# Attention in a two-layer trunk: seven of the second mixer's eight groups in a hand-written order, each taken in two parts by query tile, with the first output unit's split inside

## The chip, the cores and the metric

The kernel runs on one core of one Trainium2 chip. The metric is the device time of one execution in microseconds, taken as the median of several runs. The core has a matmul engine (PE, whose weight load shows as PEld), a vector engine (DVE), a scalar engine (ACT), GpSimd (POOL) and SyncE (SP, which here only issues DMAs). Each engine works through its own list of instructions in order and waits where an operand or a free buffer is late.

## The reference

A denoising trunk of two layers over 128 context tokens and 256 latent tokens, 1024 wide, all in float32. Each layer is a gated feed-forward half-step, a mixer, and another feed-forward half-step. The mixer of layer 0 is latent attention with 8 heads beside a convolution; that of layer 1, the second mixer, is grouped-query attention with 16 query heads of 64 over 4 key and value heads. Context tokens attend to the context alone; latent tokens attend to a cache of 128 keys and the 256 latent keys, and the kernel computes both at once.

```python
def block_attention(q, k, v, scale):
    ...
    def one(qblk):
        s = jnp.einsum('bqhgd,bshd->bhgqs', qblk, k).astype(jnp.float32) * scale
        p = jax.nn.softmax(s, axis=-1).astype(v.dtype)
        return jnp.einsum('bhgqs,bshd->bqhgd', p, v)
...
def gqa_mixer(h, w_in, g_q, g_k, w_out, ctx):
    B, S, _ = h.shape
    q, k, v = jnp.split(h @ w_in, [MIX_C, MIX_C + GQA_KV_HEADS * GQA_HEAD_DIM], axis=-1)
    q = rms_norm(q.reshape(B, S, GQA_HEADS, GQA_HEAD_DIM), g_q)
    k = rms_norm(k.reshape(B, S, GQA_KV_HEADS, GQA_HEAD_DIM), g_k)
    ...
    o = block_attention(q.reshape(B, S, GQA_KV_HEADS, grp, GQA_HEAD_DIM), keys, vals, GQA_HEAD_DIM ** -0.5)
    return o.reshape(B, S, MIX_C) @ w_out, (k, v)
```

## The kernel before, in words

All 384 tokens are worked on together, with features on the partitions. The stages follow one another: feed-forward, first mixer (`mixer_a`), two feed-forwards, second mixer (`mixer_c`), feed-forward, store.

**Dense products.** A weight matrix comes in units of 128x2048 values by DMA into a ring of three raw tiles. Each unit is split in two halves of 128x1024 into a rounded part (ACT, L162) and a remainder (DVE, L174; some units of `mixer_a` instead take ACT's L171 and a DMA that adds). Activations are split likewise: ACT casts the high part (L631), DVE subtracts it for the low part (L632). One product is then three matmuls (L264 to L266). There are four halves of each kind, so a split waits until the matmuls of an earlier unit are through. `stream` walks a list of such units: it splits up to two units ahead, calls a unit's matmuls, and after the next unit's matmuls were listed its `post`.

**Attention.** `attention` takes the heads two at a time, a group: four groups in `mixer_a`, eight in `mixer_c`. For a group of two heads the steps are:

- *scores* (L665): for each head the three query tiles of 128 rows. Tile 0 and tile 1 are latent rows against 384 keys, tile 2 is the context rows against 128. Tiles 0 and 2 of a head share one PSUM buffer, tile 1 has its own.
- *softmax*: a row maximum for each tile and head on DVE (L680, six), its product with the negated norm (L682, four), the exponentials on ACT, which also give the row sums (L685, six), and one reciprocal of all sums on DVE (L687).
- *pv*: the probabilities are turned on PE, per head four and three transposes (L703, L707) into `ps_tr` and `ps_ax` buffers, copied out by ACT (L705, 128x512) and, in `mixer_c`, by DVE (L709, 128x384); the reciprocals are turned and spread by twelve small matmul passes (L466) and copied out (L713, DVE in `mixer_c`); eight value matmuls (L719) into `ps_ax`, and DVE multiplies them by the reciprocals (L722) into a temporary `t`, which is split into `MXh` (L631) and `MXl` (L632), the input of the output product.

PSUM has four `ps_mm` buffers, two `ps_tr` and two `ps_ax`. The two heads' probabilities lie in `pr` tiles, of which `mixer_c` has four, and their turned form in `pt` tiles, of which it has two.

**Order.** A tile scheduler orders each engine's list, by the order of the program and by what it estimates to be ready; inside a `manual_schedule` block it keeps the order as written. The code before has no such block in attention. In `mixer_c` the product that makes queries, keys and values has six units. Group 0's scores and softmax come inside unit 4 (`first`), its `pv`, with group 1's scores (`ahead`) and softmax, inside unit 5 (`group`); groups 1 to 7 follow through `rest`: the scores of group g+1, then the `pv` of group g, then the softmax of group g+1. After them `out_steps` makes four units of the output product, the first two with the raw tiles loaded and split by the stream as buffers allow. In `mixer_a` all four groups go through `rest`, beside a convolution on DVE (L920) and its layer norm (L1004, L1007, L1010, L1026, L1029), which gives the other half of the input of its output product.

Of the kernel before, what the change touches and what calls it, by code (L numbers as in the profile page):

```python
# [6 lines left out]
F32 = mybir.dt.float32  # L7
# [8 lines left out]
P = 128  # L16
# [5 lines left out]
T = 384  # L22
# [57 lines left out]
class Trunk:  # L80
# [95 lines left out]
    def stream(self, steps):  # L176
        depth = {"raw": NRAW, "rawm": NRAWM}
        rest = {r: deque(s for s in steps if s.ap is not None and s.ring == r) for r in depth}
# [21 lines left out]
        done_split = set()  # L200
# [442 lines left out]
    def attention(self, heads, pairs, pool=None):  # L643

        nc = self.nc
        S = {}
        room = []

# [8 lines left out]
        def scores(hs):  # L657
            for h in hs:
                S[h] = (self.ps_mm(), self.ps_mm())
            for dst, c0, cols, q0 in ((0, 0, slice(0, T), 0), (0, T, slice(T, 512), TL), (1, 0, slice(0, T), P)):  # L660
                for h in hs:
                    qT, kT, rows = heads[h][:3]
                    kw = {"tile_position": (rows.start, 0)} if pairs else {}
                    n = cols.stop - cols.start
                    nc.tensor.matmul(S[h][dst][:, c0:c0 + n], lhsT=qT[rows, q0:q0 + P], rhs=kT[rows, cols],  # L665
                                     start=True, stop=True, **kw)

        Pm, Rm = {}, {}

        def softmax(hs):  # L670

            mx, sm = self.tb("mx", 6, 4), self.tb("sm", 6, 4)
            prs = [scratch(0, h) for h in hs]
            part = lambda h, i: (S[h][0][:, 0:T], S[h][1][:, 0:T], S[h][0][:, T:512])[i]
            off = (0, T, 2 * T, 7 * P)
            for ids in ((0, 2), (1,)):
                for j, (h, pr) in enumerate(zip(hs, prs)):
                    sc, nsc = heads[h][4], heads[h][5]
                    for i in ids:
                        nc.vector.reduce_max(out=mx[:, 2 * i + j:2 * i + j + 1], in_=part(h, i), axis=AX.X)  # L680
                    c, cj = slice(ids[0], 3, 2), slice(2 * ids[0] + j, 6, 4)
                    nc.vector.tensor_tensor(out=mx[:, cj], in0=mx[:, cj], in1=nsc[:, c], op=ALU.mult)  # L682
                    for i in ids:
                        k = slice(2 * i + j, 2 * i + j + 1)
                        nc.scalar.activation(pr[:, off[i]:off[i + 1]], part(h, i), AF.Exp, scale=sc[:, i:i + 1],  # L685
                                             bias=mx[:, k], accum_out=sm[:, k])
            nc.vector.reciprocal(sm, sm)  # L687
            Rm[hs[0]] = sm
            for h, pr in zip(hs, prs):
                S.pop(h)  # L690
                Pm[h] = pr

        def pv(hs, MXh, MXl, ps=None):

            pts = []
            for h in hs:
                pr = Pm.pop(h)
                pt = scratch(1, h).rearrange("p (a b) -> p a b", b=P)
                pts.append(pt)
                ta, tb = (ps or (self.ps_ax if h == hs[1] else self.ps_tr))(), (ps or self.ps_tr)()  # L700
                for kt in range(2):
                    for qb in range(2):
                        nc.tensor.transpose(ta[:, (2 * kt + qb) * P:(2 * kt + qb + 1) * P],  # L703
                                            pr[:, qb * T + kt * P:qb * T + kt * P + P], self.ident)
                nc.scalar.copy(pt[:, 0:4, :], ta.rearrange("p (a b) -> p a b", b=P))  # L705
                for i, o in enumerate((2 * P, T + 2 * P, 2 * T)):
                    nc.tensor.transpose(tb[:, i * P:i * P + P], pr[:, o:o + P], self.ident)  # L707
# [614 lines left out]
```

## Time and profile before

| what | value |
|---|---|
| median of three runs | 1467.29 us (1466.56 to 1467.69) |
| the profiled execution | 1467.06 us |
| its span in the trace | 1465.3 us, so 1.76 us lie around it |
| mean granted PE clock | 0.996 |
| PE busy | 1438.0 us (98%) |
| DVE busy | 1156.5 us (79%) |
| ACT busy | 667.7 us (46%) |
| groups 1 to 7 of the second mixer | about 1090 to 1140 us from the span's start |
| first matmul of the second mixer's output product | 1139.49 us |

A row of the trace's timeline gives the start, the duration, engine, line, operation, output and input, and how often it repeats without a break; behind it, in square brackets, stands how long the engine was idle before it and what ended this. Durations of one engine can overlap a little, since an instruction starts before the one ahead of it has drained; so the distance from one start to the next is what it costs in a row of equal ones. A matmul in float32 shows as two records.

### The profile page before, as it was taken

How to read it: one execution, taken by the hardware profiler on the slowest of the kernel's cores; microseconds unless marked ns; L12 is line 12 of the kernel's file. 1: busy time of each engine (PE TensorE's matmuls, PEld its weight loads, DVE VectorE, ACT ScalarE, POOL GpSimd, SP SyncE). 2: the span in 40 equal slices, each digit the busy share in tenths (PEclk: the TensorE clock that was granted, in tenths of full speed). 3: DMA queues.
4: the chain of work that ended last, by engine and by line, in shares of the span. 5: the costliest groups of instructions: out<-in, count | busy, mean ns of one | idle time of the engine just before them, and what ended most of it. 6: DMA issues, size and time to landing. Idle time of an engine off the chain costs nothing. (4 is left out here: it accounts for less than half of the span.)

```text
span 1465.3 us, 22131 instructions
## 1 busy us (share of the span) xinstructions
PE 1438.0 (98%) x8450; PEld 1397.6 (95%) x8450; DVE 1156.5 (79%) x2411; ACT 667.7 (46%) x1177; POOL 26.1 (2%) x36
## 2 busy tenths in 40 slices
PE   8999999999999999999999999999998999999997
PEld 6999999999889999999999999999976999999997
DVE  5899999959987999999779996445887698555443
ACT  4534333368776434343344333333477443333332
POOL 0000000021100000000000000000000000000000
PEclk9999999999999999999999999999999999999998
DMA  9665657699656566657565662334310263432341
GB/s 384 247 226 208 231 186 256 240 239 216 152 141 229 182 231 221 212 203 244 201 232 206 230 225 97 107 131 163 128 59 30 87 230 144 140 119 90 117 134 48
DMA packets 45066, 262.55 MB, mean 179 GB/s; under 512 B 4992, under 2 KB 6816, under 8 KB 22048
## 3 DMA queue, kind: packets, MB, share of 16 engines
q1 hardware_dynamic: 38592, 245.04, 46.6%
q0 software_dynamic: 4032, 14.16, 5.2%
q10 hardware_dynamic: 2336, 1.94, 0.4%
q8 instruction: 67, 1.10, 0.3%
q14 instruction: 39, 0.32, 0.1%
HBM read 244.98 MB, written 1.98 MB: 169 GB/s over the span
## 5 line engine op out<-in xcount | busy, mean ns | idle before, releaser
L162 ACT CAST whi<-raw 128x1024 fp32r<-128x1024 f32 (+1 forms) x346 | 327.9, 948 | 579.5 <-PE ps_mm L266 507.4
L264 PE MATMUL ps_mm<-Hh,wlo 128*128 128x386 f32 x1568 | 533.7, 340 | 0.8 <-DMA wlo<-raw 0.8
L265 PE MATMUL ps_mm<-Hl,whi 128*128 128x386 f32 x1568 | 530.6, 338 | 0.0
L266 PE MATMUL ps_mm<-Hh,whi 128*128 128x386 f32 x1568 | 529.7, 338 | 0.0
L174 DVE TENSOR_TENSOR wlo<-raw,whi 128x1024 fp32r<-128x1024 f32 (+2 forms) x318 | 346.4, 1089 | 154.5 <-ACT whi L162 152.0
L264 PEld LDWEIGHTS ps_mm<-Hh,wlo 128*128 128x128 f32 x1568 | 295.4, 188 | 3.1 <-PE ps_mm L266 1.1
L265 PEld LDWEIGHTS ps_mm<-Hl,whi 128*128 128x128 f32 x1568 | 295.8, 189 | 0.5
L266 PEld LDWEIGHTS ps_mm<-Hh,whi 128*128 128x128 f32 x1568 | 294.8, 188 | 0.0
L265 PE MATMUL ps_mm<-Gl,whi 128*128 128x384 f32 x704 | 236.7, 336 | 0.0
L264 PE MATMUL ps_mm<-Gh,wlo 128*128 128x384 f32 x704 | 236.7, 336 | 0.0
L266 PE MATMUL ps_mm<-Gh,whi 128*128 128x384 f32 x704 | 236.7, 336 | 0.0
L378 DVE SCALAR_TENSOR_TENSOR junk<-rawm,eb 128x1024 bf16<-128x1024 f32 x128 | 156.2, 1220 | 1.0 <-ACT eb L143 1.0
L378 DVE SCALAR_TENSOR_TENSOR rawm<-rawm,eb 128x1024 f32<-128x1024 f32 x128 | 156.1, 1219 | 0.3
L264 PEld LDWEIGHTS ps_mm<-Gh,wlo 128*128 128x128 f32 x704 | 132.0, 187 | 0.0
L265 PEld LDWEIGHTS ps_mm<-Gl,whi 128*128 128x128 f32 x704 | 132.0, 187 | 0.0
L266 PEld LDWEIGHTS ps_mm<-Gh,whi 128*128 128x128 f32 x704 | 132.0, 187 | 0.0
L631 ACT CAST Gh<-g 128x384 fp32r<-128x384 f32 x88 | 45.1, 512 | 89.2 <-DVE g L547 89.2
L540 ACT ACTIVATE sa<-ta,ba 128x256 f32<-128x256 f32 (+1 forms) x176 | 70.3, 447 | 3.8 <-DVE ta L537 3.7
L920 DVE SCALAR_TENSOR_TENSOR acc<-ub,vec,acc 128x399 f32<-128x399 f32 x120 | 69.8, 628 | 0.3
L547 DVE SCALAR_TENSOR_TENSOR g<-t,bb,sa 128x256 f32<-128x256 f32 (+1 forms) x176 | 65.4, 413 | 0.4 <-ACT sa L540 0.4
L485 DVE SCALAR_TENSOR_TENSOR X<-ps_mm,mod,X 128x256 f32<-128x256 f32 x88 | 32.7, 412 | 39.1 <-PE ps_mm L266 39.1
L632 DVE TENSOR_TENSOR Gl<-g,Gh 128x384 fp32r<-128x384 f32 x88 | 49.0, 557 | 12.3 <-ACT Gh L631 12.2
(276 smaller groups left out, 1285.6 us busy)
## 6 DMA issues: line engine op xcount, KB each, us to landing
raw<-wi SPq DMA_DIRECT2D x85, 1024.0 KB, 4.8
rawm<-wmt SPq DMA_DIRECT2D x64, 1024.0 KB, 4.8
raw<-wo SPq DMA_DIRECT2D x64, 704.0 KB, 4.0
wlo<-raw POOLq DMA_DIRECT2D x24, 512.0 KB, 6.3
raw<-wia SPq DMA_DIRECT2D x7, 1024.0 KB, 7.9
raw<-wic SPq DMA_DIRECT2D x6, 1024.0 KB, 4.8
raw<-wm SPq DMA_DIRECT2D x5, 1024.0 KB, 14.4
raw<-woc SPq DMA_DIRECT2D x4, 1024.0 KB, 4.9
```

Source lines behind the costliest of these rows:

```text
L162: self.nc.scalar.copy(hi, s.raw[:, c0:c1])
L174: self.nc.vector.tensor_tensor(out=lo, in0=raw, in1=hi.bitcast(F32), op=ALU.subtract)
L264: mm(out, lhsT=lo, rhs=rh, start=start, stop=False)
L265: mm(out, lhsT=hi, rhs=rl, start=False, stop=False)
L266: mm(out, lhsT=hi, rhs=rh, start=False, stop=stop)
L378: self.nc.vector.scalar_tensor_tensor(out=junk, in0=raw[:, i], scalar=1.0, in1=self.eb[:, c], op0=ALU.mult, op1=ALU.mult, accum_out=out[:, ...
L485: nc.vector.scalar_tensor_tensor(out=self.X[:, d, s0:s1], in0=ps[:, s0:s1], scalar=gate[:, d, c:c + 1], in1=self.X[:, d, s0:s1], op0=ALU.m ...
L540: nc.scalar.activation(sa[:, s0:s1], ta[:, s0:s1], AF.Silu, bias=ba[:, c:c + 1])
L547: nc.vector.scalar_tensor_tensor(out=g[:, s0:s1], in0=t2[:, s0:s1], scalar=bb[:, c:c + 1], in1=sa[:, s0:s1], op0=ALU.add, op1=ALU.mult)
L631: self.nc.scalar.copy(hi, src)
L632: self.nc.vector.tensor_tensor(out=lo, in0=src, in1=hi.bitcast(F32), op=ALU.subtract)
L920: nc.vector.scalar_tensor_tensor(out=acc[j], in0=src(t), scalar=w(t), in1=acc[j], op0=ALU.mult, op1=ALU.add)
```

## The change

`attention` is rewritten in smaller steps, each by group g and part b. Part 0 holds query tiles 0 and 2, part 1 holds tile 1: `scores(g, b)` (now L675), `maxima(g, b)` (L690, then one product L692 for both heads), `exps(g, b)` (L698), `recip(g)` (L704), `turn(g, b)` (transposes L715, copies L718), `sums(g)` (the turned reciprocals, L467, and their copy L724), `values(g)` (L734, the product L737, the cast L739), and the low part L740 that `values` hands back to be called later. Beside the order:

- part 0 is turned into `ps_tr` for both heads and copied by ACT, part 1 into `ps_ax` and copied, in `mixer_c`, by DVE; the values go to `ps_tr` (group 0 of `mixer_c`: `ps_ax`);
- the copy of the turned reciprocals goes from DVE to ACT in `mixer_c`;
- two products of maxima and norms per group stand where there were four;
- in `mixer_c` groups 1 to 7 run through `laid`, under `manual_schedule`;
- the first raw tile of the output product is loaded ahead of `laid`, and its two halves are split inside: the first at the end of group 6's turn, the second within group 7's; `stream` passes over a unit that has its tile and its halves.

`mixer_a` uses the new steps through `rest`, ordered by the tile scheduler. The lists of the feed-forwards, SP and POOL are the same as before. DVE has 32 instructions fewer, ACT 8 more, PE the same number.

```diff
+        def maxima(g, b):
...
+            for j, h in enumerate(hs):
+                for i in ids[b]:
+                    nc.vector.reduce_max(out=mx[:, i, j:j + 1], in_=part(h, i), axis=AX.X)
+            c = (slice(0, 3, 2), slice(1, 2))[b]
+            nc.vector.tensor_tensor(out=mx[:, c], in0=mx[:, c], in1=heads[hs[0]][5][:, c], op=ALU.mult)
...
+        def turn(g, b, ps=None):
+
+            for j, h in enumerate(groups[g]):
...
+                p = (ps or (self.ps_tr, self.ps_ax)[b])()
+                src = ((0, P, 2 * P, 2 * T), (T, T + P, T + 2 * P))[b]
+                for i, o in enumerate(src):
+                    nc.tensor.transpose(p[:, i * P:i * P + P], Pm[h][:, o:o + P], self.ident)
+                n = len(src)
+                copy = nc.vector.tensor_copy if pool and b else nc.scalar.copy
+                copy(pts[g][j][:, b:7:2, :], p[:, 0:n * P].rearrange("p (a b) -> p a b", b=P))
+
+        def sums(g, ps=None):
+            p = (ps or self.ps_tr)()
+            self.turn_rows(p, Rm.pop(g))
+            R = Rm[g] = self.tb("g")
+            nc.scalar.copy(R, p[:, 0:T])
+
+        def values(g, MXh, MXl, ps=None):
...
+            on = self.tb("t2")
+            nc.vector.tensor_tensor(out=on, in0=o[:, 0:T], in1=Rm.pop(g), op=ALU.mult)
+            i = heads[hs[0]][6]
+            nc.scalar.copy(MXh[:, i, :], on)
+            return lambda: nc.vector.tensor_tensor(out=MXl[:, i, :], in0=on, in1=MXh[:, i, :].bitcast(F32),
+                                                   op=ALU.subtract)
...
+        def laid(g0, MXh, MXl, unit):
+
+            low = lambda: None
+            with self.tc.manual_schedule():
+                for g in range(g0, len(groups)):
+                    more = g + 1 < len(groups)
+                    if more:
+                        scores(g + 1, 0)
+                    turn(g, 0)
+                    if more:
+                        maxima(g + 1, 0)
+                    low()
+                    sums(g)
+                    if more:
+                        exps(g + 1, 0)
+                        scores(g + 1, 1)
+                    turn(g, 1)
+                    if more:
+                        maxima(g + 1, 1)
+                    else:
+                        self.split_half(unit, 1)
+                    low = values(g, MXh, MXl)
+                    if more:
+                        exps(g + 1, 1)
+                        recip(g + 1)
+                    if g + 2 == len(groups):
+                        self.split_half(unit, 0)
+                low()
...
             self.stream(steps)
-            rest(MXh, MXl, 1)
-            self.stream(self.out_steps(a["woc"], MXh, MXl, lambda: self.mods[l, GM], nxt))
+            outs = self.out_steps(a["woc"], MXh, MXl, lambda: self.mods[l, GM], nxt)
+            outs[0].raw = self.rawp.tile([P, UN], F32, tag="raw", name="raw", bufs=NRAW)
+            nc.sync.dma_start(out=outs[0].raw, in_=outs[0].ap)
+            laid(1, MXh, MXl, outs[0])
+            self.stream(outs)
```

The lists of the engines show it at three places. First PE, from the end of one group's values to the end of the next's, in the middle of the second mixer; in each row stand the line, the operation, output and input with buffer numbers, the shape, and how many follow. `cst` is the identity, `pr` the probabilities (or, as a factor of `Vt`, their turned form), `sm` the reciprocals. Before:

```order
L665 MATMUL ps_mm<-kT_10026,qT_10024 128x384 x2
L665 MATMUL ps_mm<-kT_10026,qT_10024 128x128 x2
L665 MATMUL ps_mm<-kT_10026,qT_10024 128x384 x2
L703 MATMUL ps_tr<-cst,pr 128x128 x4
L707 MATMUL ps_tr<-cst,pr 128x128 x3
L703 MATMUL ps_ax<-cst,pr 128x128 x4
L707 MATMUL ps_tr<-cst,pr 128x128 x3
L719 MATMUL ps_ax<-pr,Vt 64x256
L466 MATMUL ps_tr<-cst,sm 64x128 x6
L719 MATMUL ps_ax<-pr,Vt 64x256 x5
L719 MATMUL ps_ax<-pr,Vt 64x128 x2
```

and in the changed kernel:

```order
L675 MATMUL ps_mm<-kT_10018,qT_10016 128x384 x2
L675 MATMUL ps_mm<-kT_10018,qT_10016 128x128 x2
L715 MATMUL ps_tr<-cst,pr 128x128 x8
L467 MATMUL ps_tr<-cst,sm 64x128 x6
L675 MATMUL ps_mm<-kT_10018,qT_10016 128x384 x2
L715 MATMUL ps_ax<-cst,pr 128x128 x6
L734 MATMUL ps_tr<-pr,Vt 64x256 x6
L734 MATMUL ps_tr<-pr,Vt 64x128 x2
```

The turned reciprocals stood behind all transposes and the first value matmul; now they stand ahead of the second half of the next group's scores, of the last six transposes and of all value matmuls.

Second ACT over the same group, up to the exponentials of the next. Before:

```order
L685 ACTIVATE pr,sm<-ps_mm,mx,sc_10030 128x384
L705 COPY pr<-ps_tr 128x512
L685 ACTIVATE pr,sm<-ps_mm,mx,sc_10030 128x128
L705 COPY pr<-ps_ax 128x512
L685 ACTIVATE pr,sm<-ps_mm,mx,sc_10030 128x384
L685 ACTIVATE pr,sm<-ps_mm,mx,sc_10030 128x128
L685 ACTIVATE pr,sm<-ps_mm,mx,sc_10030 128x384 x2
L631 CAST MXh<-t_11157 128x384
```

and in the changed kernel:

```order
L718 COPY pr<-ps_tr 128x4x128 x2
L724 COPY g<-ps_tr 128x384
L698 ACTIVATE pr,sm<-ps_mm,mx,sc_10022 128x384
L698 ACTIVATE pr,sm<-ps_mm,mx,sc_10022 128x128
L698 ACTIVATE pr,sm<-ps_mm,mx,sc_10022 128x384
L698 ACTIVATE pr,sm<-ps_mm,mx,sc_10022 128x128
L739 CAST MXh<-t_11157 128x384
L698 ACTIVATE pr,sm<-ps_mm,mx,sc_10022 128x384 x2
```

The cast of a group's result stood behind all six exponentials of the next group; now it stands ahead of the two of part 1. On DVE the reciprocal of the next group stands right behind the product that the cast reads, as it did before.

Third the end of the groups on DVE, from the product of group 6 on. Before:

```order
L722 TENSOR_TENSOR t_11234<-ps_ax,g 128x384
L687 RECIPROCAL sm<-sm 128x6
L709 COPY pr<-ps_tr 128x384
L632 TENSOR_TENSOR MXl<-t_11234,MXh 128x384
L709 COPY pr<-ps_tr 128x384
L713 COPY g<-ps_tr 128x384
L722 TENSOR_TENSOR t_11301<-ps_ax,g 128x384
```

and in the changed kernel:

```order
L737 TENSOR_TENSOR t_11232<-ps_tr,g 128x384
L704 RECIPROCAL sm<-sm 128x6
L174 TENSOR_TENSOR wlo<-raw,whi 128x1024
L740 TENSOR_TENSOR MXl<-t_11232,MXh 128x384
L718 COPY pr<-ps_ax 128x3x128 x2
L174 TENSOR_TENSOR wlo<-raw,whi 128x1024 x2
L737 TENSOR_TENSOR t_11289<-ps_tr,g 128x384
```

Three remainders of weights, the first unit's halves and one of the second unit, stand between the last two groups' products, where there was none; on ACT a cast of weights (L162) stands between the last exponentials and the copies of the last group's turned part 0.

More of the change, by code (lines that the diff above doesn't have):

```diff
@@ L177, in stream @@
         depth = {"raw": NRAW, "rawm": NRAWM}
-        rest = {r: deque(s for s in steps if s.ap is not None and s.ring == r) for r in depth}
+        rest = {r: deque(s for s in steps if s.ap is not None and s.ring == r and s.raw is None)
+                for r in depth}
         out = {r: deque() for r in depth}
@@ L199, in stream @@
         load()
-        done_split = set()
+        done_split = {id(s) for s in steps if s.parts}
         def split(s):
@@ L645, in attention @@
         nc = self.nc
-        S = {}
+        S, Pm, M, Rm, pts = {}, {}, {}, {}, {}
         room = []
+        groups = [list(range(i, i + 2)) for i in range(0, len(heads), 2)]
+        off = (0, T, 2 * T, 7 * P)
+        ids = ((0, 2), (1,))
         def scratch(i, h):
@@ L742, in rest @@
-        def rest(MXh, MXl, i0=0):
-            for i in range(i0, len(groups)):
-                ahead(i)
-                group(i, MXh, MXl)
-        return first, rest, ahead, group
+            nc.vector.tensor_tensor(out=on, in0=o[:, 0:T], in1=Rm.pop(g), op=ALU.mult)
[3 more added lines that the diff above has]
+                                                   op=ALU.subtract)
@@ new lines, in first, with ahead, soft, group @@
+        def first():
+            for b in range(2):
+                scores(0, b)
+            for b in range(2):
+                maxima(0, b)
+                exps(0, b)
+            recip(0)
+        def ahead(g):
+            for b in range(2):
+                scores(g, b)
+        def soft(g):
+            for b in range(2):
+                maxima(g, b)
+                exps(g, b)
+            recip(g)
+        def group(g, MXh, MXl, ps=None):
+            turn(g, 0, ps)
+            turn(g, 1, ps)
+            sums(g, ps)
+            values(g, MXh, MXl, ps)()
+            if g + 1 < len(groups):
+                soft(g + 1)
+            self.pop_bg(BG2)
@@ new lines, in rest @@
+        def rest(MXh, MXl):
+            for g in range(len(groups)):
+                if g + 1 < len(groups):
+                    ahead(g + 1)
+                group(g, MXh, MXl)
+        def laid(g0, MXh, MXl, unit):
[25 more added lines that the diff above has]
+                low()
@@ L749, in out_steps @@
+        return first, rest, ahead, group, laid
     def out_steps(self, w, MXh, MXl, gate, nxt):
```

105 lines of the change are left out of this document (39 added, 66 removed).

## The prediction

> **What bounds the kernel now.** The page's first part gives PE nearly the whole span, so the question for a change in one stage is where in that stage PE stands still. I read the busy time by windows, then the waits of the second mixer's groups, then the timelines of PE, DVE and ACT there.
>
> ```profile
> PE 1438.0 (98%) x8450; PEld 1397.6 (95%) x8450; DVE 1156.5 (79%) x2411; ACT 667.7 (46%) x1177; POOL 26.1 (2%) x36
> ...
> core 0: us, PE busy (x) PEld busy (x) DVE busy (x) ACT busy (x) POOL busy (x), PEclk, DMA share, GB/s
> 1099.57:1135.41 35.84, 30.48 (x269) 21.49 (x266) 27.13 (x90) 25.59 (x77) 0.00 (x0) 1.00 0.09 31
> ...
> engine line waited for: us in total, times, longest us
> ACT pr L685 <- DVE mx L682: 8.7, 6, 1.9
> PEld ps_tr L707 <- ACT pr L705: 6.4, 6, 1.5
> ```
>
> The window runs from the product L722 of group 1 to that of group 6, five groups: 35.84 / 5 = 7.17 us each, of which PE works 30.48 / 5 = 6.10. So PE is idle about 1.07 us per group, at full clock. No engine is full: a ring of waits bounds the stage. PE waits for ACT's copies (PEld's list), and ACT's exponentials for the maxima from DVE.
>
> ```profile
> 1099.57 0.55 DVE L722 TENSOR_TENSOR t<-ps_ax,g 128x384 f32<-128x384 f32 x1
> ...
> 1120.52 0.56 DVE L722 TENSOR_TENSOR t<-ps_ax,g 128x384 f32<-128x384 f32 x1 [0.78 <-PE ps_ax L719]
> 1127.97 0.56 DVE L722 TENSOR_TENSOR t<-ps_ax,g 128x384 f32<-128x384 f32 x1 [0.78 <-PE ps_ax L719]
> 1135.41 0.56 DVE L722 TENSOR_TENSOR t<-ps_ax,g 128x384 f32<-128x384 f32 x1 [0.78 <-PE ps_ax L719]
> ```
>
> The last groups repeat at 7.44 us (1127.97 to 1135.41, and 7.45 before it).
>
> **The change, part by part: the steady groups.** I follow one turn of the new lists from the start of group g's product (t = 0), with these steps:
>
> ```profile
> 1121.12 0.51 ACT L631 CAST MXh<-t 128x384 fp32r<-128x384 f32 x1 [0.47 <-DVE t L722]
> 1126.65 0.69 ACT L685 ACTIVATE pr<-ps_mm,mx,sc 128x384 f32<-128x384 f32 x1
> 1127.31 0.70 ACT L685 ACTIVATE pr<-ps_mm,mx,sc 128x384 f32<-128x384 f32 x1
> 1127.86 0.23 ACT L685 ACTIVATION_READ_ACCUMULATOR pr<-ps_mm,mx,sc 128x1 f32 x1
> 1136.54 0.52 ACT L631 CAST MXh<-t 128x384 fp32r<-128x384 f32 x1
> 1136.95 0.59 ACT L705 COPY pr<-ps_ax 128x512 f32<-128x512 f32 x1
> ...
> 1086.86 0.92 PE L665 MATMUL ps_mm<-kT,qT 64*128 64x384 f32 x4
> 1087.79 0.66 PE L703 MATMUL ps_ax<-cst,pr 128*128 128x128 f32 x4
> 1096.58 0.88 PE L466 MATMUL ps_tr<-cst,sm 128*64 128x128 f32 x12
> 1097.29 1.68 PE L719 MATMUL ps_ax<-pr,Vt 128*64 128x256 f32 x16
> 1098.90 1.78 PE L665 MATMUL ps_mm<-kT,qT 64*128 64x384 f32 x12
> ...
> 1102.85 1.01 DVE L709 COPY pr<-ps_tr 128x384 f32<-128x384 f32 x2
> 1122.13 1.21 DVE L680 TENSOR_REDUCE mx<-ps_mm 128x1 f32<-128x384 f32 x3
> 1123.26 0.15 DVE L682 TENSOR_TENSOR mx<-mx,nsc 128x2 f32<-128x2 f32 x1
> 1123.33 0.75 DVE L680 TENSOR_REDUCE mx<-ps_mm 128x1 f32<-128x128 f32 x2
> ```
>
> - The cast starts at 0.60 (1120.52 to 1121.12) and holds ACT 0.41 (1136.54 to 1136.95): 1.01.
> - Behind it in ACT's list now stand the two part-1 exponentials of group g+1. At 0.66 each (1126.65 to 1127.31) ACT is free at 2.33, the last sum read at 2.45 (1.67 + 0.55 + 0.23). Their maxima were ready before the product, so nothing else can hide this.
> - The reciprocal stands right behind the product in DVE's list and waits until 2.45; queued behind it are the maxima of group g+2 and the copies of part 1.
> - ACT's first copy of turned part 0 (0.59, 1136.95) ends at 2.92 and frees a `ps_tr` buffer, which the turned reciprocals need. PE has done the part-0 scores and eight transposes by then (1.78 for all scores, of which 0.92 fall to part 1; 1.3 for the transposes: until about 2.2) and waits.
> - Reciprocals 0.71 (1096.58 to 1097.29): 3.66. Scores of part 1, 0.93 (1086.86 to 1087.79): 4.59. Three transposes, about 0.5 by 0.66 for four: 5.1.
> - DVE has meanwhile done the four maxima (2 x 0.40 from 1.21 for three, 0.7 for the small pair) and the low part: about 4.5, no bound. Its two copies take 1.01: 6.1.
> - Values 1.61 (1097.29 to 1098.90): 7.7, the next product.
>
> So a turn takes 7.7 us against PE's 6.1. Each step waits for the one ahead of it, because the cast was moved ahead of the exponentials and the reciprocals ahead of scores, transposes and values on PE. Five turns: 38.5 - 35.84 = **+2.7**. Bounds: 6.1 a turn if no wait binds (-5.3), 8.0 if the handings-over that I set at nothing cost 0.05 at each of six (+4.2). I take 7.7, since each step has a row of its own form. From group 0 to group 1 the lists change in both ways; I take **0**, with -1.3 (7.44 to PE's 6.1) and +0.3 (7.44 to 7.7) as ends.
>
> **The end of the groups.**
>
> ```profile
> 1139.49 0.44 PE L264 MATMUL ps_mm<-MXh,wlo 128*128 128x384 f32 x1
> ...
> 1098.34 1.22 DVE L174 TENSOR_TENSOR wlo<-raw,whi 128x1024 fp32r<-128x1024 f32 x1
> 1099.47 0.18 DVE L478 TENSOR_TENSOR rsw<-r 128x24 f32<-128x24 f32 x1
> ...
> 432.72 1.06 ACT L171 ACTIVATE wlo<-raw 128x1024 fp32r<-128x1024 f32 x1
> 433.69 0.95 ACT L1007 ACTIVATE ub<-acc 128x399 f32<-128x399 f32 x2
> ```
>
> Before, the output product starts 4.08 us after group 6's product (1135.41 to 1139.49). Now: exponentials until 2.33; the cast of 128x1024 weights, 0.97 by L171 of that shape on ACT: 3.30; copy 0.59: 3.89; reciprocals 0.71: 4.6; three transposes 0.5: 5.1; DVE's copies 1.01: 6.1 (L174, 1.13 by its step, and the low part end at about 4.9, ahead of them); values 1.61: 7.7. Three matmuls of the output product stand ahead of the values, bounded above by 3 x 0.44; I take 0.5 off: 7.2 - 4.1 = **+3.1**, with 1.5 (only the weight cast and a copy added, 0.97 + 0.59) and 3.6 as ends. The other two weight remainders delay group 7's product, 2.3 us at 1.13 each; the output product needs it only behind seven other inputs, which hides this.
>
> **What leaves unit 5.**
>
> ```profile
> 1071.44 1.05 ACT L162 CAST whi<-raw 128x1024 fp32r<-128x1024 f32 x1 [3.12 <-PE ps_tr L266]
> 1078.00 1.13 PE L665 MATMUL ps_mm<-kT,qT 64*128 64x384 f32 x4 [1.17 <-ACT pr L685]
> ```
>
> In the lists before, weight casts (1.05 each) and remainders of the output product lie inside units 4 and 5; ahead of `laid` they are gone there. PE's wait of 1.17 for exponentials shrinks; I take **-0.9**, between -1.5 and 0.
>
> **The first mixer.**
>
> ```profile
> 438.34 1.06 ACT L171 ACTIVATE wlo<-raw 128x1024 fp32r<-128x1024 f32 x1 [2.77 <-PE ps_tr L264]
> 440.82 1.29 ACT L1029 ACTIVATE g<-ta,vec 128x384 f32<-128x384 f32 x2
> ...
> 442.56 0.98 PE L264 MATMUL ps_mm<-MXh,wlo 128*128 128x384 f32 x4 [3.16 <-ACT MXh L631]
> ...
> core 0: us, PE busy (x) PEld busy (x) DVE busy (x) ACT busy (x) POOL busy (x), PEclk, DMA share, GB/s
> 444.00:447.40 3.40, 3.40 (x13) 3.40 (x12) 1.03 (x2) 1.89 (x4) 0.00 (x0) 0.51 0.93 199
> ```
>
> PE waits 3.16 us for the layer norm's chain. DVE loses eight products L682 at 0.07 (1123.26 to 1123.33), 0.56; on ACT the L171 of 432.72 no longer parts the four squares L1007 (0.97). So the chain comes up to 1.0 sooner. But L162 and L171 now stand ahead of L1029 and wait for PE's buffers until 438.34: 438.34 + 2 x 0.97 = 440.28, against 440.82: 0.54. I take **-0.7** between these. Ends: +0.5 if the splits come half a step later, -2.6 if the wait shortens enough to spare the slow stretch behind it. That stretch is a clock of 0.51 for 3.4 us, so 3.40 x 0.49 = 1.67 lost. The other edits (copies by other shapes, `ps_tr` for values) change a buffer's name, no work.
>
> Sum: -0.7 - 0.9 + 0 + 2.7 + 3.1 = +4.2 on the profiled 1467.06, which is 0.23 under the median: 1471.26, so **1471.5** as a median.
>
> **Rivals.** *The clock falls at the end of the groups.* PE is done with group 7's part-0 transposes at about 1.2 and waits until 3.9: 2.7 us idle in one piece. The 3.16 us wait at 442.56 was followed by a clock of 0.51; a price of 1.67 gives 1473.2, and with a turn of 8.0 about 1474.7. Against it: 2.7 is shorter, and 1.07 per group leaves the clock at 1.00. The Trainium skill, "TensorE: Matmul & The Clock Gate", section "What's actually happening", says the clock halves after an idle window of about 3.4 us that runs free of the kernel. The trace agrees only in that the clock fell after a wait and to a half; 3.16 is below that figure. By that rule the 2.7 would not do it, and the forecast stands.
>
> *The rhythm stays.* The new ring may lose on ACT what it wins in earlier maxima: 7.44 a turn as in the last groups would be 5 x 7.44 = 37.2, +1.4; the end at its low bound, +1.5; first mixer and unit 5 at -0.7 - 0.9 - 1.0 (a head that gains): +0.3, 1467.6. For it speaks that before, too, reciprocal and copies close the ring; against it, that the cast's 1.0 us now lies inside it.
>
> *Faster: PE becomes the bound.* If the part-1 exponentials end by about 1.6, so that ACT's copy is out at 2.2 when PE has its transposes done, PE does not wait for reciprocals; the copies of part 1 then have to hide too. A turn is 6.1: 5 x 6.1 - 35.84 = -5.3; with +1.5 at the end and -1.6 elsewhere -5.4: 1461.9. Against it: both idle pieces, 0.7 ahead of the reciprocals and 0.5 ahead of the values, have to go, and the first is 0.7 short.
>
> **How the numbers follow.** Chances: the forecast 0.51 (1469.5 to 1473.5 by its own terms), the clock or longer turns 0.15, the rhythm that stays 0.22, PE-bound 0.12. This kernel's measurement tells about 0.2%, 2.9 us, from no change: faster is below 1464.4, slower above 1470.2. Slower: 0.15 and 0.45 of the forecast, 0.60; same: 0.22 and the forecast's low end, 0.28; faster: 0.12. The range is 1465.5 to 1475.0: it takes in the rhythm that stays and most of the clock's case, and leaves out PE-bound.
>
> **What would show it.** Right: products L737 of the middle groups 7.7 apart; in them ACT's cast, then two exponentials, then the reciprocal at about 2.4; PE idle ahead of L467 with ACT's L718 as releaser, and ahead of L734 with DVE's L718; three matmuls of the output product ahead of group 7's values, and the rest of it from about 7.7 us behind group 6's product. Wrong: turns below 7.4, or PE busy 6.1 of each; a granted clock of 0.5 after the end's wait; a shorter or vanished wait before the first mixer's second half of outputs beyond 1 us.

## The result, and the profile after

The changed kernel takes 1477.06 us (median of six runs, 1473.08 to 1478.84), the kernel before 1467.03 (six runs, 1466.43 to 1468.77). The medians lie 10.0 us apart; the ratio is 1.0064, 95% interval 1.0054 to 1.0074, so 0.64% or some 9.4 us slower. The forecast of a slower kernel held, its size did not: 1471.5 was said, with a range up to 1475.0. The runs of the changed kernel lie further apart than those before; the mean granted clock of the fastest is 0.998, of the profiled one 0.993, and the granted clock turns out to be a part of the cause.

The profiled execution took 1478.78 us (span 1477.0), 11.7 over that of before. These are starts of the same events in both timelines; X is the residual sum, which each stage updates at its end.

| event | before | after | later by |
|---|---|---|---|
| first update of X, first feed-forward | 224.58 | 225.08 | 0.50 |
| first update of X behind the first mixer's stage (second feed-forward) | 664.02 | 665.62 | 1.60 |
| product of group 0 in the second mixer | 1092.13 | 1093.20 | 1.07 |
| product of group 1 | 1099.57 | 1101.31 | 1.74 |
| product of group 6 | 1135.41 | 1141.79 | 6.38 |
| first update of X by the output product | 1147.74 | 1159.94 | 12.20 |
| first update of X, last feed-forward | 1372.15 | 1383.86 | 11.71 |

So 0.5 us come at the very start, where nothing was changed (this event lies between 224.3 and 225.5 in all profiles of this study), 1.1 in the stretch with the first mixer, -0.5 up to group 0, 0.7 in the first turn, 4.6 in the five steady turns and 5.8 at the end of the groups; 0.5 us is given back in the output product.

A turn is the stretch from one group's product (L737) to the next. The page's first line, and the busy time and waits of the five steady turns (groups 1 to 6), in the profile after:

```profile
PE 1443.2 (98%) x8450; PEld 1401.0 (95%) x8450; DVE 1152.4 (78%) x2379; ACT 671.2 (45%) x1185; POOL 26.0 (2%) x36
...
core 0: us, PE busy (x) PEld busy (x) DVE busy (x) ACT busy (x) POOL busy (x), PEclk, DMA share, GB/s
1101.31:1141.79 40.48, 33.58 (x272) 22.40 (x273) 23.90 (x66) 27.35 (x80) 0.00 (x0) 1.00 0.01 1
...
engine line waited for: us in total, times, longest us
DVE sm L704 <- ACT pr L698: 9.5, 5, 1.9
PE ps_tr L467 <- ACT pr L718: 4.8, 5, 1.0
```

DVE's reciprocal waits 1.9 us in every turn for the exponentials, and PE waits 1.0 for ACT's copy ahead of the turned reciprocals: the two waits that the prediction named. One turn in the timelines of the three engines, in the order of the chain:

```profile
1117.50 0.56 DVE L737 TENSOR_TENSOR t<-ps_tr,g 128x384 f32<-128x384 f32 x1 [0.77 <-PE ps_tr L734]
1118.09 0.51 ACT L739 CAST MXh<-t 128x384 fp32r<-128x384 f32 x1 [2.14 <-DVE t L737]
1119.95 0.19 DVE L704 RECIPROCAL sm<-sm 128x6 f32<-128x6 f32 x1 [1.90 <-ACT pr L698]
1120.45 0.87 PE L467 MATMUL ps_tr<-cst,sm 128*64 128x128 f32 x12 [0.97 <-ACT pr L718]
1121.25 0.92 PE L675 MATMUL ps_mm<-kT,qT 64*128 64x384 f32 x4
1122.10 0.87 PE L715 MATMUL ps_ax<-cst,pr 128*128 128x128 f32 x6
1122.68 1.02 DVE L718 COPY pr<-ps_ax 128x384 f32<-128x384 f32 x2 [0.58 <-PE ps_ax L715]
1123.39 2.10 PE L734 MATMUL ps_tr<-pr,Vt 128*64 128x256 f32 x16 [0.41 <-DVE pr L718]
1125.59 0.56 DVE L737 TENSOR_TENSOR t<-ps_tr,g 128x384 f32<-128x384 f32 x1 [0.77 <-PE ps_tr L734]
```

Every link is there, and the turn is 8.10 us, not 7.7. The end of the groups:

```profile
1141.79 0.56 DVE L737 TENSOR_TENSOR t<-ps_tr,g 128x384 f32<-128x384 f32 x1 [0.77 <-PE ps_tr L734]
1144.11 1.03 ACT L162 CAST whi<-raw 128x1024 fp32r<-128x1024 f32 x1
1145.68 1.55 PE L467 MATMUL ps_tr<-cst,sm 128*64 128x128 f32 x12 [2.56 <-ACT pr L718]
1152.48 0.56 DVE L737 TENSOR_TENSOR t<-ps_tr,g 128x384 f32<-128x384 f32 x1 [0.91 <-PE ps_tr L734]
...
1143.12:1145.68 2.56, 0.00 (x0) 0.00 (x1) 0.70 (x2) 2.56 (x7) 0.00 (x0) 0.87 0.00 0
1145.68:1152.36 6.68, 6.68 (x38) 4.72 (x38) 4.57 (x6) 3.75 (x5) 0.00 (x0) 0.54 0.13 26
```

The last two rows are windows with the columns of the table above; the third number from the end is the granted clock. The idle piece of 2.56 us is there as worked out (2.7), but behind it the clock is at a half: 2.56 x 0.13 + 6.68 x 0.46 = 3.4 us of clock missing, so about 6.8 us at half speed. The turned reciprocals take 1.55 instead of 0.87, and the last turn takes 10.69.

And the first mixer's wait:

```profile
439.63 1.05 ACT L162 CAST whi<-raw 128x1024 fp32r<-128x1024 f32 x1 [1.06 <-PE ps_tr L267]
440.58 1.05 ACT L171 ACTIVATE wlo<-raw 128x1024 fp32r<-128x1024 f32 x1
441.54 1.29 ACT L1088 ACTIVATE g<-ta,vec 128x384 f32<-128x384 f32 x2
443.29 1.65 PE L265 MATMUL ps_mm<-MXh,wlo 128*128 128x384 f32 x4 [3.36 <-ACT MXh L632]
```

It did not shrink: 3.36 us, before 3.16.

### The profile page after: what moved, and what is told of

Its sections match the earlier page's. It is cut to its first block, busy times and chain, and to the rows that moved or that the text cites. A ratio compares the mean times of both kernels' runs of the same rounds, so it can differ in the third digit from the quotient of the medians.

```text
span 1477.0 us, 22113 instructions
## 1 busy us (share of the span) xinstructions
PE 1443.2 (98%) x8450; PEld 1401.0 (95%) x8450; DVE 1152.4 (78%) x2379; ACT 671.2 (45%) x1185; POOL 26.0 (2%) x36
## 5 line engine op out<-in xcount | busy, mean ns | idle before, releaser
L162 ACT CAST whi<-raw 128x1024 fp32r<-128x1024 f32 (+1 forms) x346 | 327.6, 948 | 577.9 <-PE ps_mm L267 506.4
L267 PE MATMUL ps_mm<-Hh,whi 128*128 128x386 f32 x1568 | 529.7, 338 | 0.0
L267 PEld LDWEIGHTS ps_mm<-Hh,whi 128*128 128x128 f32 x1568 | 294.8, 188 | 0.0
L267 PE MATMUL ps_mm<-Gh,whi 128*128 128x384 f32 x704 | 236.7, 336 | 0.0
L267 PEld LDWEIGHTS ps_mm<-Gh,whi 128*128 128x128 f32 x704 | 132.0, 187 | 0.0
```

The lines of the kernel that those rows point to most:

```text
L162: self.nc.scalar.copy(hi, s.raw[:, c0:c1])
L267: mm(out, lhsT=hi, rhs=rh, start=False, stop=stop)
```

## The experiments

The theory after the first look: in the steady turns a ring of waits closes over the cast that was moved ahead of the exponentials; at the end an ACT cast of weights makes PE idle long enough for the clock to fall; the first mixer gained nothing. Each kernel is compared with the kernel before, run on the same chip.

**The cast moved back, alone.**

```diff
-                    low = values(g, MXh, MXl)
+                    cast, low = values(g, MXh, MXl, late=True)
                     if more:
                         exps(g + 1, 1)
                         recip(g + 1)
+                    cast()
```

> The changed kernel, with one thing moved back: the cast of a group's result (L739) again stands behind the two part-1 exponentials of the next group on ACT, and no longer ahead of them. My theory is that this cast closes the ring which sets the turn of 8.10 us (1125.59 to 1133.69 between products L737): exponentials 1.0 us late, reciprocal, ACT's copy, turned reciprocals, part-1 scores and transposes, DVE's copies, values. It expects turns of 7.3 (the reciprocal ready 0.7 us into a turn instead of 2.45; PE then reaches the turned reciprocals at about 2.2 instead of 2.95), five turns 4 us shorter, about 1.3 us less at the end, and 1470 (1468 to 1473) as a time. The rival: the turn is set by what stands between DVE's copies of part 1 and the product (copies 1.0, values 2.0), wherever the cast stands; it expects 8.0 to 8.1 a turn and 1477.

Measured: 1469.82 us, ratio 1.0016 (1.0006 to 1.0025). The turns, in the timeline of this kernel:

```profile
1115.81 0.56 DVE L737 TENSOR_TENSOR t<-ps_tr,g 128x384 f32<-128x384 f32 x1 [0.77 <-PE ps_tr L734]
1116.52 0.19 DVE L704 RECIPROCAL sm<-sm 128x6 f32<-128x6 f32 x1 [0.16 <-ACT pr L698]
1118.08 0.88 PE L467 MATMUL ps_tr<-cst,sm 128*64 128x128 f32 x12 [0.29 <-ACT pr L718]
1121.03 2.10 PE L734 MATMUL ps_tr<-pr,Vt 128*64 128x256 f32 x16 [0.42 <-DVE pr L718]
1123.23 0.56 DVE L737 TENSOR_TENSOR t<-ps_tr,g 128x384 f32<-128x384 f32 x1 [0.76 <-PE ps_tr L734]
```

The reciprocal comes 0.71 us into the turn, PE's wait ahead of L467 falls from 0.97 to 0.29, and a turn takes 7.42 (7.3 was expected). The rival, that copies and values set the turn wherever the cast stands, falls. Only the turn from group 0 to group 1 is as long as in the change, 8.11 us (1092.85 to 1100.96). The last turn took 7.25, and the clock stayed at 1.00 there, behind a wait of 1.25 us:

```profile
1140.67 0.87 PE L467 MATMUL ps_tr<-cst,sm 128*64 128x128 f32 x12 [1.25 <-ACT pr L718]
```

**The turned reciprocals later on PE.** With them ACT's copy of them (L724) moves behind the exponentials of part 0.

```diff
-                    sums(g)
                     if more:
-                        exps(g + 1, 0)
                         scores(g + 1, 1)
+                    if more:
+                        exps(g + 1, 0)
                     turn(g, 1)
+                    sums(g)
```

> The changed kernel with the turned reciprocals (L467) moved on PE from ahead of the next group's part-1 scores to behind the last six transposes, so that they stand right ahead of the values; the cast stays ahead of the exponentials, and ACT takes the part-0 exponentials ahead of the copy of the turned reciprocals. Theory of the ring: any link taken out shortens it; PE has 3.5 us of scores and transposes to do while the reciprocal is late, the turned reciprocals come at 3.5 and the values at about 5.5, behind DVE's copies; turns of 7.2 to 7.4, and 1471. Rival (only the cast matters): the late reciprocal only moves the wait to the new place, 8.0 a turn and 1477.

Measured: 1471.74 us, ratio 1.0029 (1.0015 to 1.0044).

```profile
1114.81 0.56 DVE L737 TENSOR_TENSOR t<-ps_tr,g 128x384 f32<-128x384 f32 x1 [0.77 <-PE ps_tr L734]
1117.26 0.19 DVE L704 RECIPROCAL sm<-sm 128x6 f32<-128x6 f32 x1 [1.89 <-ACT pr L698]
1118.92 0.88 PE L467 MATMUL ps_tr<-cst,sm 128*64 128x128 f32 x12
1120.02 2.10 PE L734 MATMUL ps_tr<-pr,Vt 128*64 128x256 f32 x16 [0.22 <-DVE pr L718]
1122.23 0.56 DVE L737 TENSOR_TENSOR t<-ps_tr,g 128x384 f32<-128x384 f32 x1 [0.77 <-PE ps_tr L734]
```

The reciprocal is as late as in the change (1.89 us of waiting on DVE), yet PE no longer waits for it, and the turn is again 7.42. So it was a ring: the late cast is one link, the early place of the turned reciprocals another, and taking out either gives the same turn. What is left in both is PE's wait for DVE's copies.

The end of the groups is not as in the run before, though. The last turn takes 10.16 us (1137.08 to 1147.24): the scheduler sets six matmuls of the output product ahead of the last values, and here too the clock fell, for one stretch of 3.4 us, though no single wait of PE ahead of it was longer than 0.87 us (the last row is a window, columns as above):

```profile
1138.90 1.20 PE L715 MATMUL ps_ax<-cst,pr 128*128 128x128 f32 x6 [0.55 <-ACT pr L698]
1140.97 1.21 PE L467 MATMUL ps_tr<-cst,sm 128*64 128x128 f32 x12 [0.87 <-ACT pr L718]
...
1141.36:1144.77 3.41, 3.41 (x17) 2.48 (x14) 2.83 (x5) 2.60 (x5) 0.00 (x0) 0.50 0.00 0
```

**No split of weights inside.**

```diff
-                    else:
-                        self.split_half(unit, 1)
...
-                    if g + 2 == len(groups):
-                        self.split_half(unit, 0)
```

> The changed kernel without the splits of the first output unit inside the hand-written order; its raw tile is still loaded ahead, and the stream splits it behind. In the profile the last turn takes 10.69 us (1141.79 to 1152.48), with the ACT cast of weights 0.97 ahead of the copies, PE idle 2.56 us and a clock of 0.50 behind it. Theory (weight casts inside the last turn cost about 3 us, of which the clock adds 2.6): the turn to group 7's product falls to about 7.5, PE's idle pieces stay under 1.5 us, the clock stays at 1.00 there; 2 to 5 us less than the changed kernel, 1473. Rival: the splits have to be done somewhere and the output product then waits for them behind the values; the same 1477, with a wait of 2 to 3 us for L162 or L174 at the first output matmul.

Measured: 1471.21 us, ratio 1.0030 (1.0019 to 1.0040), with turns of 8.10 as in the change and 7.45 for the last. More than the idle piece went, as PE's timeline of the last turn shows:

```profile
1139.95 0.42 PE L265 MATMUL ps_mm<-MXh,wlo 128*128 128x384 f32 x1
...
1142.60 0.34 PE L265 MATMUL ps_mm<-MXh,wlo 128*128 128x384 f32 x1
1142.87 0.88 PE L467 MATMUL ps_tr<-cst,sm 128*64 128x128 f32 x12
```

Left to the stream, the first output unit's weights are split earlier (casts L162 at 1080.38 and 1085.90, inside unit 5, where the change has them from 1144.11 on), and the scheduler puts matmuls of the output product into the very place where PE waited for the exponentials. In the change only three of them stand ahead of the last values. So the splits inside kept the output product out of PE's waits. The turn from group 0 to group 1 is shorter as well, 7.10 us (1092.13 to 1099.23) where the change has 8.11. The rival, a wait of 2 to 3 us for the splits behind the values, did not come.

**PE kept busy in the last turn.**

```diff
+                for _ in range(4 if pool and g + 1 == len(groups) and not b else 1):
-                for i, o in enumerate(src):
-                    nc.tensor.transpose(p[:, i * P:i * P + P], Pm[h][:, o:o + P], self.ident)
+                    for i, o in enumerate(src):
+                        nc.tensor.transpose(p[:, i * P:i * P + P], Pm[h][:, o:o + P], self.ident)
```

> The changed kernel with the eight part-0 transposes of the last group done four times over (the same values to the same place), which gives PE 2.6 us of work in the idle piece of 2.56 us at 1143.1. Nothing that ACT or DVE does changes. Theory (the idle piece makes the clock fall to a half for two stretches of 3.4 us, and this costs 2.6 us of the end): clock 1.00 from 1143 to 1152, the last turn 8.1 to 8.3 us instead of 10.69, 1474.5. Rival (the clock follows something else, or the end does not hang on PE): clock 0.5 there as before or the same length of the turn, 1477.

Measured: 1475.11 us (four runs, 1474.17 to 1477.76), ratio 1.0056 (1.0041 to 1.0071). The windows of the last turn (columns as above):

```profile
1141.00:1146.00 5.00, 4.64 (x46) 4.23 (x46) 2.18 (x4) 3.74 (x8) 0.00 (x0) 1.00 0.00 0
1146.00:1149.20 3.20, 3.20 (x25) 2.57 (x25) 3.00 (x5) 3.20 (x4) 0.00 (x0) 1.00 0.02 5
```

The clock stays at 1.00, with ACT and DVE doing the same as in the change, and the last turn takes 8.55 us (1141.18 to 1149.73) instead of 10.69. So the clock falls because PE is idle, and it cost 2.1 us of that turn. The time confirms it only loosely: the two ratios' intervals overlap, and the changed kernel's own runs spread over 5.8 us.

**The first mixer alone.** The new parts in the first mixer; the second mixer as before.

> The new parts in the first mixer alone; the second mixer keeps the code of before. My prediction had -0.7 for this part. The traces since then show the splits L162 and L171 ahead of the layer norm's L1088 only start when PE's last matmul frees their buffers (439.63 in the changed kernel), so that the reordering ahead of them is lost: this theory expects +0.1 to +0.2 with one half-clock stretch behind the wait and +1.1 with two, as in most profiles of the new code, so 1467.5 to 1468.8. The prediction's reading expects 1466.3.

Measured: 1466.74 us against 1467.19, ratio 0.9998 (0.9989 to 1.0007): no difference that can be told. The -0.45 lies between the two expectations (-0.9, and +0.3 to +1.6), and the interval of 1.3 us to either side leaves both open in size; what it excludes is that this part explains the loss. In this profile one stretch of half clock followed the wait (from the first update of X to the one behind this mixer it is 439.95 us, in the profile before 439.44); in that of the changed kernel there were two.

**The ring opened.** No weight split stands inside, and the body of the hand-written loop becomes:

```diff
+                    if more:
+                        scores(g + 1, 0)
+                    turn(g, 0)
+                    if more:
+                        maxima(g + 1, 0)
+                        scores(g + 1, 1)
+                        exps(g + 1, 0)
+                    turn(g, 1)
+                    if more:
+                        maxima(g + 1, 1)
+                    sums(g)
+                    low()
+                    if more:
+                        exps(g + 1, 1)
+                    cast, low = values(g, MXh, MXl, late=True)
+                    if more:
+                        recip(g + 1)
+                    cast()
```

> The changed kernel with the hand-written order rewritten so that no link of the ring is left on the path: on PE both parts of the next group's scores and both parts' transposes stand ahead of the turned reciprocals and the values; on ACT the six exponentials of the next group stand ahead of the cast; no weight split inside. The theory of the ring expects PE as the bound: 6.1 to 6.3 us a turn (PE's own work is 6.1), 0.9 us less per turn than before's mean of 7.17, and 1461 (1459 to 1463), 0.4% under the kernel before. The rival, that DVE (5.4 us of work a turn and in the middle of every handing-over) bounds the stage whatever the order, expects turns of 6.8 and more and 1466.

Measured: 1460.29 us, ratio 0.9957 (0.9943 to 0.9970). The same kernel was run a second time:

> The opened ring once more, unchanged, beside the run with the filled wait on the same chip: 1460.3 as before, and the clock at 0.5 for 3.4 or 6.8 us behind the first mixer's wait.

Measured: 1460.46 us, ratio 0.9957 (0.9945 to 0.9970). The five turns, in the profile of the first of the two:

```profile
1098.22:1129.50 31.28, 31.28 (x272) 22.10 (x273) 24.77 (x68) 27.70 (x83) 0.00 (x0) 1.00 0.01 2
...
1115.00 1.88 PE L734 MATMUL ps_tr<-pr,Vt 128*64 128x256 f32 x16
```

31.28 / 5 = 6.26 us a turn, and PE shows no idle time: it is the bound, with the same matmuls as in the change. The rival that DVE bounds the stage falls. The turn from group 0 to group 1 takes 6.10 us. This version beats both kernels.

**The same parts, ordered by the scheduler.**

```diff
-            laid(1, MXh, MXl, outs[0])
+            rest(MXh, MXl, 1)
```

> The new parts with the second mixer's groups 1 to 7 left to the tile scheduler instead of the hand-written order, and the first raw tile loaded ahead as in the change. It tells the parts from the order. If the order is to blame for the loss, turns are 6.5 to 7.2 and the time 1464 (1462 to 1467); if the parts themselves cost (the copy of the turned reciprocals on ACT, values in the same two buffers as the transposes), turns are 7.4 to 8.1 and the time is 1470 or more.

Measured: 1467.35 us, ratio 1.0000 (0.9991 to 1.0008). The middle turns take 7.51 us (products at 1106.20, 1113.71 and 1121.22), those of before 7.44.

Neither expectation is met in full: the parts do not cost, but under the scheduler they do not gain either. With the same steps, the scheduler's order gives the time before, the change's order loses 9 us with the splits inside and 4.4 without (the run without a split), and the opened one gains 7.

**The ring opened, the first mixer as before.**

> As the run with the opened ring, with the first mixer's attention as before. If the first mixer's new order is worth +0.2 and up to +1.1 with the clock, this one lies 0 to 1 us under that run: 1460.5. It should be the fastest of all.

Measured: 1460.79 us, ratio 0.9956 (0.9944 to 0.9969), which cannot be told from the time with the new first mixer. It is not the fastest of all, as was expected, but fits the run of the first mixer alone.

**The splits later in the last turn.**

```diff
                     turn(g, 1)
                     if more:
                         maxima(g + 1, 1)
-                    else:
-                        self.split_half(unit, 1)
+                    if not more:
+                        self.split_half(unit, 0)
+                    if not more:
+                        self.split_half(unit, 1)
...
-                    if g + 2 == len(groups):
-                        self.split_half(unit, 0)
```

> The changed kernel with both splits of the first output unit placed in the last group's turn, behind the copies of its turned parts; the order of all other steps as in the change, so turns of 8.10 us. Theory: what costs at the end is the place of one ACT cast of weights (0.97) ahead of the last group's copies, because it stretches PE's idle piece from 1.6 to 2.6 us and with it the clock falls. It expects PE idle 1.6 to 1.8 us, clock 1.00, the last turn 8.3 to 8.7 us (DVE's remainders stand ahead of the last product) instead of 10.69, and 1474 (1473 to 1475). Rival: splits inside the hand-written order cost wherever they stand, since ACT or DVE must do them while the last group waits: 10 us and more for the turn and 1477.

Measured: 1475.25 us (1473.15 to 1476.3), ratio 1.0046 (1.0032 to 1.0060); the last turn takes 8.59. The idle piece is as short as expected, but the clock falls all the same, for half as long:

```profile
1143.25 1.40 PE L467 MATMUL ps_tr<-cst,sm 128*64 128x128 f32 x12 [1.61 <-ACT pr L718]
...
1143.00:1146.00 3.00, 2.75 (x18) 2.14 (x18) 0.86 (x2) 2.00 (x4) 0.00 (x0) 0.58 0.00 0
1146.00:1149.00 3.00, 2.90 (x20) 2.27 (x20) 2.92 (x5) 2.95 (x4) 0.00 (x0) 0.86 0.02 5
```

3.00 x 0.42 + 3.00 x 0.14 = 1.7 us of clock missing, 3.4 us at half speed. So the place of the two splits decides on 2.1 us of the last turn in these two profiles, 1.7 of it by one stretch of half clock in place of two, and the expectation that 1.6 to 1.8 us of idling leaves the clock at 1.00 was wrong.

**The ring opened, with the splits inside.** The first at the end of group 6's turn, the second at the end of the last.

> The run with the opened ring, with the two splits inside again, the first at the end of group 6's turn, the second at the end of the last turn. With the ring open ACT and DVE have room, so the place of the splits should hardly matter: turns of 6.25 us, the clock at 1.00, and 1460.3 to 1462. If the split inside costs by itself, as in the changed kernel, the last turn grows by 2 us and more, and the time is 1463 or above.

Measured: 1462.7 us, ratio 0.9965 (0.9953 to 0.9978): faster than before by 5 us. Without the splits the median was 2.4 us lower, but on another chip; by the ratios it is 1.2 us, and the intervals overlap. In the profile the last turn takes 6.14 us (1130.44 to 1136.58) instead of 4.55 (1129.50 to 1134.05), and the turn from group 0 to group 1 takes 7.27 (1091.89 to 1099.16) instead of 6.10. Between the two expectations: the profile shows that the splits cost inside, the times alone would not settle it, and turns of 6.26 are untouched.

**The first mixer's wait filled.**

```diff
             r = self.spread(None, st["r"])
+            idle = self.ps_ax()
+            for _ in range(12):
+                nc.tensor.matmul(idle[:, 0:TL], lhsT=self.ident, rhs=acc[0][:, 0:TL], start=True, stop=True)
```

> The run with the opened ring, with twelve matmuls more in the first mixer, whose result nobody reads, in PE's wait of 3.36 us ahead of the output product's second half (some 2.9 us of work by 0.24 each). Theory: in every profile so far that wait was followed by a clock of 0.5 for 3.4 or 6.8 us; it is PE's idleness that lowers it. With PE busy the clock stays at 1.00 there and the time falls by 1.7 us at least against the same kernel without them (3.4 us at half clock), to 1458.6. Rival: the clock there follows something else (the DMA share of 0.9 and more in the same stretch), it falls as before and the time is that of the repeat, or above by what the filling delays.

Measured: 1460.52 us against 1460.46 for the same kernel without them. The clock did what was expected, the time did not. First the filled wait, then the same window of the kernel without the filling:

```profile
438.99 5.35 PE L1087 MATMUL ps_ax<-acc,cst 128*128 128x256 f32 x24
...
core 0: us, PE busy (x) PEld busy (x) DVE busy (x) ACT busy (x) POOL busy (x), PEclk, DMA share, GB/s
444.00:447.40 3.40, 3.40 (x21) 3.37 (x20) 1.12 (x2) 1.46 (x3) 0.00 (x0) 1.00 0.74 148
```

```profile
444.00:447.40 3.40, 3.40 (x17) 3.40 (x16) 1.12 (x3) 1.71 (x4) 0.00 (x0) 0.74 0.80 166
```

The clock stays at 1.00 at a DMA share of 0.74, near the 0.80 of the kernel without the filling, so it follows PE's idleness and not the DMAs. But a matmul of this form takes 0.42 us, not 0.24; the filling lasts 5.35 us, holds up the output product by 1.2 us or so (443.99 against 442.80), and so eats most of what the clock gives back (the half clock ran from 442.80 to 445.74 with PE at work, 1.5 us lost). A shorter filling was not tried.

## Why the prediction was wrong in size

**Steady turns: the mechanism right, the term mis-sized.** The step "a turn takes 7.7 us" measured 8.10, so "38.5 - 35.84 = +2.7" became 40.48 - 35.84 = +4.6. The links came as worked out up to the reciprocal (2.45 us into the turn by the forecast and in the trace) and to the turned reciprocals (2.92 and 2.95). What was short: DVE's second copy ends 6.20 us into the turn, where 6.1 was said (the turned reciprocals take 0.80 and not 0.71); PE's values end 1.72 us behind it (the next scores start at 1125.42), where 1.61 was said, although the values of group 0, whose copies are long done, do take 1.61 (1091.40 to 1093.01); and from there to the product pass another 0.17 us (1125.59), a handing-over set at nothing. The bound of 8.0 had allowed 0.05 for each of six.

**Group 0 to 1: 0 was wrong.** The first turn takes 8.11 us, +0.7 against 7.44, and the upper end, +0.3, was built on a turn of the ring. By the timeline it is not the ring: the turned reciprocals start 2.45 us into this turn (1095.65) and PE does not wait for them. PE waits ahead of the values, 0.93 us where the steady turns have 0.41, for DVE's copies, which stand in DVE's list behind a row of small steps for a norm (L475 to L1200, from 1095.46 on):

```profile
1098.40 1.01 DVE L718 COPY pr<-ps_ax 128x384 f32<-128x384 f32 x2
1099.10 2.10 PE L734 MATMUL ps_tr<-pr,Vt 128*64 128x256 f32 x16 [0.93 <-DVE pr L718]
```

The runs agree. No exponentials of group 1 stand behind the cast here, they were done in unit 5, so with the cast moved back this turn stays at 8.11 us while the steady ones fall to 7.42. With the turned reciprocals behind the last transposes, so that DVE's copies come earlier, it is 7.27 (1092.70 to 1099.97). Without the splits inside it is 7.10 while the steady turns stay at 8.10: a part of this turn's scores and transposes then stands ahead of group 0's product, in unit 5; why the splits decide this was not followed up.

**End of the groups: the structure right, the clock wrong.** Without the clock's fall the output product goes on 8.03 us behind group 6's product (1141.18 to 1149.21 in the filled last turn); less 0.5 for the three matmuls done ahead and 4.1 for before, +3.4, where +3.1 was forecast. The step that failed is "2.7 would not do it": the rival "the clock falls at the end of the groups" was given 1.67 us and a chance within 0.15, and it came in the profiled execution, for two stretches and not one. In the change the output product goes on 10.57 us behind (1141.79 to 1152.36), 2.5 us more.

**Unit 5: right in sign.** -0.5 (1.60 to 1.07 in the table of events), -0.9 was forecast, inside its bounds. The reason holds: with the splits back in the stream (no split inside, and the opened ring) the stretch is 428.0 us long, as before (428.1), and 427.6 in the change.

**The first mixer: the failed step is "wait for PE's buffers until 438.34".** That time is the release of an L171, which in the row quoted waits for a matmul L264. The cast L162, which stands first now, waits for L267, the last of the three: 439.63 in the changed kernel. It and an L171 (440.58) run ahead of L1088, which starts at 441.54, and the 0.5 us won ahead are lost. Of the 1.1 us in that stretch of the profiled execution most is the second stretch of half clock; alone, the part makes no difference that can be measured.

**The rivals.** The rhythm that stays was wrong for this order, and is what the scheduler made of the same parts (1467.35). PE as the bound, given 0.12, did not happen in the change, since both idle pieces stayed (0.97 and 0.41); with both taken out it happened as the rival had it, 6.26 us a turn where 6.1 was said, and 1460.3.

The sum by what was measured: 0.5 + 1.1 - 0.5 + 0.7 + 4.6 + 5.8 - 0.5 = 11.7 on the profiled execution, where -0.7 - 0.9 + 0 + 2.7 + 3.1 = 4.2 was forecast. Of the 7.5 us between them 2.7 lie at the end of the groups, most of it by the clock, 1.9 in the steady turns and 1.8 in the first mixer. The clock's share is in part chance, as the last section shows, and the direction of the forecast rested on the turns and the end, which were right in kind.

## What to carry to other kernels

An order written by hand is worth what its ring of waits is worth: follow one turn through all engines, and move the steps that nobody waits for (here the cast of a result and the split of weights) behind those that the next turn needs. Taking out one link of two gave the same 7.42 us; only with every link off the path did PE become the bound, and with the splits of weights back in the stream the same steps went from 9 us of loss to 7 us of gain. And a step sized from a row of the same form still leaves out the handing-over between engines: of 8.1 us a turn 0.4 went unseen, 0.17 of it between PE's last value matmul and DVE's product.

## What the runs showed of the hardware

Waits of PE much shorter than the 3.16 us seen before can halve its clock, and the length of the single wait does not decide it. In the profiles the clock changes on a grid of 3.41 us, as windows of 1 us show: in the changed kernel it falls at 441.90 and at 1145.04, and 703.14 us are 206 steps of 3.413; in the run with the turned reciprocals later it falls at 441.64 and 1141.36, 205 steps; in the run with the later splits at 443.72 and 1143.46, 205 steps. These are windows of that grid at the end of the groups, in the changed kernel (two), with the later splits, with the turned reciprocals later, and with the cast moved back (columns as above):

```profile
1141.63:1145.04 3.41, 1.27 (x9) 0.82 (x8) 0.75 (x2) 2.66 (x6) 0.00 (x0) 1.00 0.00 0
1145.04:1148.45 3.41, 2.77 (x19) 2.44 (x19) 2.04 (x3) 2.25 (x5) 0.00 (x0) 0.50 0.00 0
...
1140.04:1143.45 3.41, 1.57 (x14) 1.04 (x14) 1.18 (x3) 2.55 (x7) 0.00 (x0) 1.00 0.00 0
...
1137.95:1141.36 3.41, 1.88 (x18) 1.17 (x18) 1.09 (x2) 3.41 (x8) 0.00 (x0) 1.00 0.00 0
...
1138.22:1141.63 3.41, 1.93 (x21) 1.31 (x19) 2.08 (x4) 2.92 (x7) 0.00 (x0) 1.00 0.00 0
```

PE is idle for 2.14, 1.84 and 1.53 us of the three windows that half clock followed, and for 1.48 of the one behind which the clock stayed at 1.00. So these four go by the idle time summed within one window and not by the longest single wait (0.87 us in the third, 1.25 in the last); a wait cut in two by a boundary would then count less in each window. A sharp limit is not shown: at the end of the kernel before, half clock followed a window with 1.38 us of idle time as well (1454.27 to 1457.68). On the way back the second row had 0.64 us of idle time and a second stretch of half clock followed; with 0.10 us, in the run with the later splits, one stretch was enough. Filling the wait kept the clock at 1.00 in both places where this was tried.

The Trainium skill, "TensorE: Matmul & The Clock Gate", section "What's actually happening", has the fall after an idle window of about 3.4 us, and says that the window runs free of the kernel. The traces agree with the length, 3.413 us, and with windows that run free, since the grid lies at another place in most of the profiles: the first mixer's fall comes between 441.64 and 443.92, and in the opened ring, which was profiled twice, at 442.84 and at 442.34, where PE's wait ends at 442.65 and 442.80. They do not agree with an idle window, since 1.53 us of idle time in one were enough, and the measurement decides. That executions of the changed kernel differ by a stretch, as their clocks from 0.993 to 0.998 suggest, would fit this, but only one of them was profiled.

PE's busy time is not PE's work: the same 272 records count 33.58 us in the change's five turns and 31.28 in the opened ring. By groups of equal shape 2.0 us of this lie in the values (13.2 us busy against 11.2): in the change they start at 1123.39 and wait inside their stage for DVE's second copy, which ends at 1123.70, without a gap in the rows.
